# Block 5's low-half top-k search: from sign sums on ScalarE to counts on VectorE

## The chip, the cores and the metric

The kernel runs on one core of a Trainium2 chip. The metric is the device time of one execution in microseconds (us); smaller is better. The engines are TensorE (PE, matmul), VectorE (DVE), ScalarE (ACT), GpSimd (POOL) and SyncE (SP, which issues most DMAs).

## What is computed

One decoder layer over 1024 tokens of width 1024: a mixer of sparse attention and a gated short convolution, then a mixture of 32 experts with two per token. What matters here is the sparse attention. For each block of 128 query rows an indexer gives a score for every admissible key, and only the 256 best keys of each row take part in the softmax:

```python
score = jnp.where(admissible[None], score.astype(jnp.float32), -jnp.inf)
_, idx = lax.top_k(score, top_k)          # top_k = 256
...
logits = jnp.where(valid[:, :, None, None, :], logits, -jnp.inf)
p = jax.nn.softmax(logits, axis=-1)
```

Blocks 0 and 1 have at most 256 admissible keys and need no choice. Block t (2 to 7) has rows of 128 (t + 1) scores.

## The kernel before

The stages follow one another on TensorE: the projections and the indexer's scores (to about 190 us), twelve convolution columns and eight gate tiles (`conv_in`, `conv_out`, `gconv_tile`, to about 428 us), the attention of blocks 0 to 7, with the other gates' matmuls as filling (to about 640 us), the merge and the router, then the experts.

**The search.** `topk` does not sort. It finds the 256th largest score of each row as a bit pattern and then turns the score tile into a bias of 0 or -1e30. It has four steps: a 16-bit key from the upper half of each score; a descent over 16 bits on that key ("th"); the same on the lower half ("tl") among the scores whose upper half equals the one found; and the finish, which builds the threshold, breaks ties by a running count, and writes the bias over the scores. One bit of a descent counts, for each row, the keys at or above a candidate and moves the candidate up or down.

There are two searches. The vector search (blocks 2, 3, 4: 384, 512 and 640 scores) counts on VectorE with a compare that sums (line 357), then three short operations on [128, 3] tiles (lines 370 to 373). The tiles `acc` and `over` of these lie in PSUM, in a tile of tag "pv", which has one buffer. The scalar search (blocks 5, 6, 7: 768, 896 and 1024 scores) takes on ScalarE the sum of the signs of key minus candidate (line 328), and two one-column operations per block move the candidate (lines 343 and 347). Its keys, its finish and the preparation between the halves run on VectorE. The finish (lines 405 to 424) is VectorE's; its last operation, the write-back of the bias (line 426), is ScalarE's.

**Who sets the order.** In the convolution and gate stage the order of TensorE, VectorE and ScalarE is the order in which the program writes the instructions (`manual_schedule`). Both searches are generators. Ahead of each piece of work they yield its engine and an estimate of its length, and `search(us)` (line 430) takes pieces until the credit of the engines is used up:

```python
left = {n: us * SHARE[n] + searches.get(n, 0.0) for n in SHARE}
for name in ("scalar", "vector"):
    while name in searches:
        gen, step = searches[name]
        if step is not None:
            if left[step[0]] <= 0:
                break
            left[step[0]] -= step[1]
        step = next(gen, None)
```

An overdraft is carried to the next call, unused credit is not. `proj_col` calls `search(2.8)` in the middle and at the end of each of its two chains of 24 matmuls (four calls per column, none in the columns 0 and 1), and `gconv_tile` once more after each of its two up-projections, ahead of the gate product of line 530: six calls per gate tile. `SHARE` is 0.72 for VectorE, and for ScalarE 0.6 in the convolution part and 0.68 from the gate tiles on. What is left after the last call is written by one `search(1.0e6)` behind the stage, outside the fixed order and at low priority (`prio(LATE)`): the planner puts it where an engine has nothing else.

**After it.** In the attention only TensorE's order is fixed by hand; VectorE and ScalarE are ordered by the planner. `att_probs` reads the bias of its block, `att_values` transposes the probabilities, splits them into the tiles `ph` and `pl` (tag "pt", four buffers, which it shares with the search's `junk`, `signs` and the keys of blocks 6 and 7), and multiplies by the values into the PSUM tile `o`, which has the tag "pv" too.

Of the kernel before, what the change touches and what calls it, by code (L numbers as in the profile page):

```python
# [9 lines left out]
F32 = mybir.dt.float32  # L10
F32R = mybir.dt.float32r
I16 = mybir.dt.int16
U16 = mybir.dt.uint16
I32 = mybir.dt.int32
AF = mybir.ActivationFunctionType
OP = mybir.AluOpType
AX = mybir.AxisListType

P = 128
# [8 lines left out]
TOPK = 256  # L28
LN_EPS = 1e-5
ALPHA = 2.0 ** 0.25  # L30
NEG = -1.0e30
# [47 lines left out]
def build(tc, I, out):  # L79
    nc = tc.nc  # L80
# [73 lines left out]
    def psf(name, shape=(P, 512), tag="f", dt=F32):  # L154
        return ps.tile(list(shape), dt, name=name, tag=tag, bufs={"f": 2, "l": 3, "tr": 2, "pv": 1}[tag])
# [84 lines left out]
    for t in range(NB):  # L240
# [12 lines left out]
        c = slice(t * P, (t + 1) * P)  # L253
# [8 lines left out]
    score = {}  # L262
    w = load_nat("w_qi", 512, "wwcc")
    for t in range(2, NB):
# [8 lines left out]
        L = (t + 1) * P  # L273
        sc = kv.tile([P, L], F32, name=f"score{t}")
        score[t] = sc
        for h in range(NH):
            for n0 in range(0, L, 512):
# [8 lines left out]
                else:  # L286
                    nc.vector.scalar_tensor_tensor(sc[:, n0:n1], rl, wis[:, t, h:h + 1], sc[:, n0:n1],  # L287
                                                   op0=OP.mult, op1=OP.add)
# [12 lines left out]
    junk = part("junk", [P, S], "pt", 4, U16)  # L301
    keys = kv.tile([P, 18 * P], U16, name="keys")

    def topk(blocks, scalar=False):
        ng = len(blocks)
        V = nc.vector

        def tmp(name, dt=F32):
            return const.tile([P, ng], dt, name=f"{name}{blocks[0]}")

        cnt, acc, neg, sg, off, need = [tmp(n) for n in ("cnt", "acc", "neg", "sg", "off", "need")]
        if not scalar:
            pa = psf("acc", (P, 2 * ng), "pv")
            acc, over = pa[:, :ng], pa[:, ng:]
        hi, lo, msk = [tmp(n, I32) for n in ("thi", "tlo", "msk")]
        L = [(t + 1) * P for t in blocks]
        if scalar:
            key = [keys[:, 12 * P:12 * P + n] if n == 6 * P else part("key", [P, S], "pt", 4, U16)[:, :n] for n in L]
            signs = part("signs", [P, S], "pt", 4, I16)
            scratch = signs.bitcast(U16)  # L320
        else:
            key = [keys[:, sum(L[:i]):sum(L[:i + 1])] for i in range(ng)]
            scratch = junk

        def sign_sums(dt, b, o):
            for i in range(ng):
                yield "act", 0.45 + L[i] / 1000
                nc.scalar.activation(signs[:, :L[i]], key[i].bitcast(dt), AF.Sign, bias=b[:, i:i + 1], scale=1.0,
                                     accum_out=o[:, i:i + 1])

        def descend_signs(name, base, dt, above=None):

            c, b, total, sign, least = [tmp(name + n) for n in ("", "b", "s", "g", "l")]
            V.memset(b, 0.5 - (base + 32768.0))
            for i in range(ng):
                if above is None:
                    V.memset(least[:, i:i + 1], L[i] - 511.0)
                else:
                    V.tensor_scalar(least[:, i:i + 1], above[:, i:i + 1], 2.0 * L[i] - 511.0, None, op0=OP.add)
            for bit in range(15, -1, -1):  # L340
                yield from sign_sums(dt, b, total)
                for i in range(ng):
                    nc.scalar.activation(sign[:, i:i + 1], total[:, i:i + 1], AF.Sign, bias=least[:, i:i + 1],
                                         scale=1.0)
                if bit:
                    for i in range(ng):
                        nc.scalar.activation(b[:, i:i + 1], sign[:, i:i + 1], AF.Identity, bias=b[:, i:i + 1],
                                             scale=-float(1 << bit) / 2)
            yield "act", 2.0
            yield "act", 0.0  # L350
            V.scalar_tensor_tensor(c, sign, 0.5, b, op0=OP.mult, op1=OP.subtract)
            return c

        def count(op, dt, c, o):
            for i in range(ng):
                yield "dve", 0.4 + L[i] / 1000
                V.tensor_scalar(junk[:, :L[i]], key[i].bitcast(dt), c[:, i:i + 1], None, op0=op, op1=OP.add,
                                accum_out=o[:, i:i + 1])

        def descend(name, base, dt, above=None):  # L360
            if scalar:
                return (yield from descend_signs(name, base, dt, above))
            c = tmp(name)
            if above is not None:
                V.tensor_copy(over, above)
            V.memset(c, base + 32768.0)
            for bit in range(15, -1, -1):
                yield from count(OP.is_ge, dt, c, cnt)
                if above is not None:
                    V.tensor_tensor(cnt, cnt, over, op=OP.add)  # L370
                step = float(1 << bit)
                V.tensor_scalar(acc, cnt, TOPK - 0.5, step, op0=OP.is_ge, op1=OP.mult)
                V.scalar_tensor_tensor(c, acc, -step / 2 if bit else -1.0, c, op0=OP.add, op1=OP.add)
            return c

        for i, t in enumerate(blocks):
            yield "dve", L[i] / 500
            h = score[t].bitcast(I16)[:, 1::2]
            m = scratch[:, :L[i]].bitcast(I16)
            V.tensor_scalar(m, h, 0.0, 32767.0, op0=OP.is_lt, op1=OP.mult)  # L380
            V.tensor_tensor(key[i].bitcast(I16), h, m, op=OP.bitwise_xor)
        th = yield from descend("th", -32768.0, I16)
        above = tmp("above")
        if scalar:
            V.tensor_scalar(acc, th, -1.0, -0.5, op0=OP.mult, op1=OP.add)
            yield from sign_sums(I16, acc, above)
            yield "act", 2.0
            yield "act", 0.0
        else:
            yield from count(OP.is_gt, I16, th, above)  # L390
        V.tensor_scalar(neg, th, 0.0, None, op0=OP.is_lt)
        V.tensor_scalar(sg, neg, -2.0, 1.0, op0=OP.mult, op1=OP.add)
        V.tensor_scalar(off, neg, 65535.0, None, op0=OP.mult)
        for i, t in enumerate(blocks):
            low = score[t].bitcast(U16)[:, 0::2]
            yield "dve", L[i] / 400
            V.tensor_scalar(scratch[:, :L[i]], low, sg[:, i:i + 1], off[:, i:i + 1], op0=OP.mult, op1=OP.add)
            V.scalar_tensor_tensor(key[i], key[i].bitcast(I16), th[:, i:i + 1], scratch[:, :L[i]], op0=OP.is_equal,
                                   op1=OP.mult)
        if scalar:  # L400
            yield "act", 2.0
            yield "act", 0.0
        tl = yield from descend("tl", 0.0, U16, above)
        yield "dve", 1.5
        V.tensor_copy(hi, th)
        V.tensor_scalar(msk, neg, 32767.0, None, op0=OP.mult)
        V.tensor_tensor(hi, hi, msk, op=OP.bitwise_xor)
        V.tensor_scalar(hi, hi, 16, None, op0=OP.logical_shift_left)
        V.tensor_tensor(tl, tl, sg, op=OP.mult)
        V.tensor_tensor(lo, tl, off, op=OP.add)  # L410
        V.tensor_tensor(hi, hi, lo, op=OP.bitwise_or)
        for i, t in enumerate(blocks):
            s = score[t]
            T = hi.bitcast(F32)[:, i:i + 1]
            jk, cm = scratch[:, :L[i]], key[i]
            yield "dve", L[i] / 300
            V.tensor_scalar(jk, s, T, None, op0=OP.is_gt, op1=OP.add, accum_out=cnt[:, i:i + 1])
            V.tensor_scalar(jk, s, T, None, op0=OP.is_equal)
            yield "dve", L[i] / 300
            V.tensor_scalar(need[:, i:i + 1], cnt[:, i:i + 1], -1.0, float(TOPK), op0=OP.mult, op1=OP.add)  # L420
            V.tensor_tensor_scan(cm, jk, jk, 0.0, op0=OP.add, op1=OP.bypass)
            yield "dve", L[i] / 300
            V.scalar_tensor_tensor(cm, cm, need[:, i:i + 1], jk, op0=OP.is_le, op1=OP.mult)
            V.scalar_tensor_tensor(s, s, T, cm, op0=OP.is_gt, op1=OP.add)
            yield "act", L[i] / 800
            nc.scalar.activation(s, s, AF.Copy, bias=NEG, scale=-NEG)

    searches = {}

    def search(us):  # L430

# [266 lines left out]
    for i in range(FILLEND):  # L698
        const_w = MINFILL if i >= 8 else MINFILL0
        if i < len(units):  # L700
            L = (units[i][0] + 1) * P
# [121 lines left out]
    V = nc.vector  # L823
# [196 lines left out]
    raw, parts, xT, gu, act, hT = {}, {}, {}, {}, {}, {}  # L1020
# [397 lines left out]
def pack(inputs):  # L1418
# [4 lines left out]
    def tiled(m):  # L1423
        return c(m.reshape(-1, P, m.shape[1]).transpose(1, 0, 2))

    o = {}
    o["x"] = c(a["x"][0])
    o["xt"] = tiled(a["x"][0].T)
    o["w_q"] = tiled(w[:, 0:512])
# [12 lines left out]
    o["w_out"] = tiled(a["w_out"][0])  # L1442
    o["gate_bias"] = c(a["gate_bias"][0].reshape(16, P).T)
    o["conv_w"] = c(a["conv_w"][0].reshape(3, 4, P).transpose(2, 1, 0))
# [30 lines left out]
```

## Time and profile before

| | us |
|---|---|
| median of 3 runs (1473.53 to 1477.25) | 1474.6 |
| the profiled execution | 1478.14 |
| its span, first to last instruction | 1476.3 |
| TensorE busy | 1399.8 (95%) |
| VectorE busy | 1092.0 (74%) |
| ScalarE busy | 996.0 (67%) |
| GpSimd busy | 395.1 (27%) |

All rows of the trace are of the one profiled execution, and times within it count from the start of its span. A row of a timeline gives the start, the length, the engine, the line, the operation and its tiles, and in brackets how long the engine stood idle before it and what released it. A row of a group gives the busy time in total, the mean of one in ns, and the idle time before. The granted clock of TensorE is given as a share of full speed.

### The profile page before, as it was taken

How to read it: one execution, taken by the hardware profiler on the slowest of the kernel's cores; microseconds unless marked ns; L12 is line 12 of the kernel's file. 1: busy time of each engine (PE TensorE's matmuls, PEld its weight loads, DVE VectorE, ACT ScalarE, POOL GpSimd, SP SyncE). 2: the span in 40 equal slices, each digit the busy share in tenths (PEclk: the TensorE clock that was granted, in tenths of full speed). 3: DMA queues.
4: the chain of work that ended last, by engine and by line, in shares of the span. 5: the costliest groups of instructions: out<-in, count | busy, mean ns of one | idle time of the engine just before them, and what ended most of it. 6: DMA issues, size and time to landing. Idle time of an engine off the chain costs nothing.

```text
span 1476.3 us, 20415 instructions
## 1 busy us (share of the span) xinstructions
PE 1399.8 (95%) x6746; PEld 1154.8 (78%) x6746; DVE 1092.0 (74%) x1917; ACT 996.0 (67%) x1657; POOL 395.1 (27%) x343
## 2 busy tenths in 40 slices
PE   8999999999979999998999799999999999999993
PEld 7888688878867888886887688888887787777772
DVE  5354699995066666677526799999999888888876
ACT  5453468779936766675323488888888788778864
POOL 2442113232224555541000212211111111111106
PEclk9999999999989999999999699999999999999997
DMA  5211111122121121247746688999999999999942
GB/s 197 72 43 57 59 57 44 46 84 79 44 85 58 58 72 65 86 165 251 273 160 240 251 290 320 369 370 369 359 365 360 357 354 360 366 358 363 365 188 115
DMA packets 97054, 301.78 MB, mean 204 GB/s; under 512 B 14671, under 2 KB 19151, under 8 KB 96945
## 3 DMA queue, kind: packets, MB, share of 16 engines
q1 hardware_dynamic: 88160, 284.28, 52.3%
q0 software_dynamic: 8784, 16.16, 4.3%
q8 instruction: 54, 0.88, 0.2%
q14 instruction: 56, 0.45, 0.1%
HBM read 276.12 MB, written 40.11 MB: 214 GB/s over the span
## 4 chain that ended last, share of the span: by engine, by line
PE 66%; DMA 15%; DVE 9%; ACT 5%; issue 3%; POOL 1%; SPq 0%; ACTq 0%; DVEq 0%; POOLq 0%
DMA er<-in_w_e 13%; PE pc L148 6%; PE pc L150 6%; PE pc L149 6%; PE gu L148 4%; PE gu L150 4%; PE gu L149 4%; PE pj L148 2%; PE pj L149 2%; PE pj L150 2%; PE py L1113 2%; PE py L1117 2%; PE py L1114 2%; PE pv L664 2%; DVE el L139 2%
## 5 line engine op out<-in xcount | busy, mean ns | idle before, releaser
L139 DVE TENSOR_TENSOR el<-er,eh 128x1024 fp32r<-128x1024 f32 x376 | 442.9, 1220 | 47.1 <-ACT eh L135 44.6
L135 ACT ACTIVATE eh<-er 128x1024 fp32r<-128x1024 f32 x376 | 385.9, 1062 | 48.8 <-PE gu L150 17.4
L148 PE MATMUL gu<-eh,exh 128*128 128x512 f32 x512 | 209.0, 408 | 0.0
L150 PE MATMUL gu<-eh,exl 128*128 128x512 f32 x512 | 203.4, 397 | 0.0
L149 PE MATMUL gu<-el,exh 128*128 128x512 f32 x512 | 203.2, 397 | 0.0
L148 PE MATMUL pc<-xh,ch 128*128 128x512 f32 x448 | 178.8, 399 | 0.0
L150 PE MATMUL pc<-xh,cl 128*128 128x512 f32 x448 | 175.7, 392 | 0.0
L149 PE MATMUL pc<-xl,ch 128*128 128x512 f32 x448 | 175.4, 392 | 0.0
L1134 POOL DMA_INDIRECT y_d<-yo,gidx x29 | 46.1, 1588 | 436.5 <-ACT yo L1126 421.9
L150 PEld LDWEIGHTS gu<-eh,exl 128*128 128x128 f32 x512 | 96.8, 189 | 23.8 <-DVE exl L139 0.5
L148 PEld LDWEIGHTS gu<-eh,exh 128*128 128x128 f32 x512 | 97.1, 190 | 20.7 <-ACT exh L135 0.4
L149 PEld LDWEIGHTS gu<-el,exh 128*128 128x128 f32 x512 | 97.1, 190 | 20.4
L139 POOL TENSOR_TENSOR cl<-cr,ch 128x1024 fp32r<-128x1024 f32 x28 | 68.1, 2431 | 134.4 <-ACT ch L135 115.2
L1114 PE MATMUL py<-el,hT 128*128 128x512 f32 x256 | 101.3, 396 | 0.0
L1113 PE MATMUL py<-eh,hT 128*128 128x512 f32 x256 | 101.3, 396 | 0.0
L150 PEld LDWEIGHTS pc<-xh,cl 128*128 128x128 f32 x448 | 84.5, 189 | 18.1
L645 POOL TENSOR_TENSOR p<-p,mx 128x128 f32<-128x128 f32 (+7 forms) x64 | 74.8, 1179 | 82.0 <-DVE mx L644 75.3
L148 PEld LDWEIGHTS pc<-xh,ch 128*128 128x128 f32 x448 | 84.7, 189 | 13.5 <-ACT rl L283 0.4
L149 PEld LDWEIGHTS pc<-xl,ch 128*128 128x128 f32 x448 | 84.7, 189 | 13.4
L287 DVE SCALAR_TENSOR_TENSOR score<-rl,wis,score 128x512 f32<-128x512 f32 (+1 forms) x70 | 53.6, 779 | 44.8 <-ACT rl L283 43.7
L1117 PE MATMUL py<-eh,hT 128*128 128x512 f32 x256 | 80.3, 395 | 0.0
L283 ACT ACTIVATE rl<-sc 128x512 f32<-128x512 f32 (+1 forms) x80 | 41.1, 524 | 53.7 <-PE sc L281 41.3
(338 smaller groups left out, 3032.4 us busy)
## 6 DMA issues: line engine op xcount, KB each, us to landing
er<-in_w_e SPq DMA_DIRECT2D x384, 512.0 KB, 11.1
cr<-in_w_ct SPq DMA_DIRECT2D x28, 512.0 KB, 3.5
gc_d<-g SPq DMA_DIRECT2D x8, 512.0 KB, 2.6
ga_d<-g SPq DMA_DIRECT2D x8, 512.0 KB, 2.6
gg<-ga_d SPq DMA_DIRECT2D x16, 256.0 KB, 4.0
gg<-gc_d SPq DMA_DIRECT2D x16, 256.0 KB, 4.4
wor<-in_w_out SPq DMA_DIRECT2D x8, 512.0 KB, 5.4
xn<-in_x SPq DMA_DIRECT2D x8, 512.0 KB, 4.8
```

What stands on the lines that cost most here:

```text
L135: exps["last"] = nc.scalar.activation(hi, src, AF.Copy).ins
L139: i = eng.tensor_tensor(lo, src, hi.bitcast(F32), op=OP.subtract)
L148: nc.tensor.matmul(ps, sh, mh, start=start, stop=False)
L149: nc.tensor.matmul(ps, sh, ml, start=False, stop=False)
L150: return nc.tensor.matmul(ps, sl, mh, start=False, stop=stop).ins
L283: nc.scalar.activation(rl, a, AF.Relu)
L287: nc.vector.scalar_tensor_tensor(sc[:, n0:n1], rl, wis[:, t, h:h + 1], sc[:, n0:n1], op0=OP.mult, op1=OP.add)
L645: nc.gpsimd.tensor_tensor(p[:, :L], p[:, :L], mx[:, 0:1].to_broadcast([P, L]), op=OP.mult)
L1113: nc.tensor.matmul(py[n], hT[e][:, 0, k], hi[k][:, cs], start=k == 0, stop=False)
L1114: nc.tensor.matmul(py[n], hT[e][:, 0, k], lo[k][:, cs], start=False, stop=False)
L1117: nc.tensor.matmul(py[n], hT[e][:, 1, k], hi[k][:, cs], start=False, stop=k == 3)
L1134: nc.gpsimd.indirect_dma_start(out=y_d, out_offset=bass.IndirectOffsetOnAxis(ap=si, axis=0), in_=yo, in_offset=None, bounds_check=S - 1, o ...
```

## The change

The low half of block 5's search leaves the scalar search. `descend_signs` and `sign_sums` get a first block `i0`, and the low half now runs with `i0 = 1`, for blocks 6 and 7 alone. A new `descend_one` does block 5's low half by counts on VectorE, one column wide, with `acc` and `over` in a PSUM tile of tag "pv" and `junk` as the output of its compare. The finish becomes a function `finish(tl, i0, i1, scratch)` over a range of blocks. The scalar search appends a generator `first_alone` (block 5's counts and finish) to a list, and the vector search runs it after its own finish. The upper half of block 5 stays on ScalarE.

```diff
+        def descend_one(base, dt, above, c):
+
+            pa = psf("acc", (P, 2), "pv")
+            acc, over = pa[:, 0:1], pa[:, 1:2]
+            cnt, c = tmp("cnt1")[:, 0:1], c[:, 0:1]
+            V.tensor_scalar(over, above[:, 0:1], float(L[0]), 0.5, op0=OP.add, op1=OP.mult)
+            V.memset(c, base + 32768.0)
+            for bit in range(15, -1, -1):
+                yield "dve", 0.7 + L[0] / 1000
+                V.tensor_scalar(junk[:, :L[0]], key[0].bitcast(dt), c, None, op0=OP.is_ge, op1=OP.add,
+                                accum_out=cnt)
+                V.tensor_tensor(cnt, cnt, over, op=OP.add)
+                step = float(1 << bit)
+                V.tensor_scalar(acc, cnt, TOPK - 0.5, step, op0=OP.is_ge, op1=OP.mult)
+                V.scalar_tensor_tensor(c, acc, -step / 2 if bit else -1.0, c, op0=OP.add, op1=OP.add)
...
-        tl = yield from descend("tl", 0.0, U16, above)
-        yield "dve", 1.5
...
+        def finish(tl, i0, i1, scratch):
+            r = slice(i0, i1)
+            yield "dve", 1.5
...
+            for i in range(i0, i1):
...
+                yield "dve", L[i] / 300
...
+                yield "act", L[i] / 800
+                nc.scalar.activation(s, s, AF.Copy, bias=NEG, scale=-NEG)
+
+        if not scalar:
+            tl = yield from descend("tl", 0.0, U16, above)
+            yield from finish(tl, 0, ng, scratch)
+            yield from shared[0]
+            return
+
+        def first_alone():
+            tl = tmp("tf")
+            yield from descend_one(0.0, U16, above, tl)
+            yield from finish(tl, 0, 1, junk)
+
+        shared.append(first_alone())
+        tl = yield from descend_signs("tl", 0.0, U16, above, 1)
+        yield from finish(tl, 1, ng, scratch)
 
-    searches = {}
+    searches, shared = {}, []
```

## Rows read from the trace of the kernel before

**Rows 1.** Page, section 2: busy tenths in 40 slices, TensorE and VectorE.

```profile
PE   8999999999979999998999799999999999999993
...
DVE  5354699995066666677526799999999888888876
```

**Rows 2.** Busy us by stretch: length, PE, PEld, DVE, ACT, POOL; clock, DMA, GB/s.

```profile
352.00:409.00 57.00, 57.00 (x258) 47.11 (x257) 5.18 (x11) 52.83 (x134) 15.28 (x11) 1.00 0.17 62
...
431.00:442.00 11.00, 3.28 (x9) 2.04 (x9) 9.95 (x26) 4.23 (x12) 3.54 (x4) 0.57 0.34 119
...
440.00:450.00 10.00, 8.52 (x35) 6.98 (x36) 6.15 (x29) 4.50 (x14) 4.88 (x9) 0.69 0.00 0
```

**Rows 3.** TensorE's timeline around the hole: start, length, operation, wait and releaser.

```profile
434.51 0.48 PE L633 MATMUL lg<-kT,qT 128*128 128x128 f32 x1 [3.89 <-DVE mx L635]
...
439.93 0.47 PE L672 MATMUL tr<-identr,p 128*128 128x128 f32 x1 [3.34 <-POOL p L645]
...
442.21 0.58 PE L664 MATMUL pv<-ph,vhl 128*128 128x256 f32 x1 [0.15 <-ACT ph L135]
```

**Rows 4.** VectorE's timeline in the same stretch, long operations.

```profile
425.28 0.69 DVE L530 TENSOR_TENSOR g<-pu,g 128x512 f32<-128x512 f32 x1 [6.62 <-PE pu L150]
...
428.00 3.38 DVE L423 SCALAR_TENSOR_TENSOR key<-key,need,signs 128x896 uint16<-128x896 uint16 x1
...
431.31 0.68 DVE L530 TENSOR_TENSOR g<-pu,g 128x512 f32<-128x512 f32 x1
...
431.91 1.14 DVE L424 SCALAR_TENSOR_TENSOR score<-score,thi,key 128x896 f32<-128x896 f32 x1
...
432.96 1.27 DVE L417 TENSOR_SCALAR_CACHE_REDUCE signs<-score,thi 128x1024 uint16<-128x1024 f32 x1
...
435.91 2.28 DVE L421 TENSOR_TENSOR_SCAN key<-signs 128x1024 uint16<-128x1024 uint16 x1
...
439.65 1.30 DVE L424 SCALAR_TENSOR_TENSOR score<-score,thi,key 128x1024 f32<-128x1024 f32 x1
```

**Rows 5.** ScalarE: write-backs of blocks 3, 4, 2 (timeline); block 5's low sums (groups).

```profile
345.27 0.61 ACT L426 ACTIVATE score<-score 128x512 f32<-128x512 f32 x1
...
351.56 0.74 ACT L426 ACTIVATE score<-score 128x640 f32<-128x640 f32 x1 [2.50 <-DVE score L424]
...
406.77 0.52 ACT L426 ACTIVATE score<-score 128x384 f32<-128x384 f32 x1
...
L328 ACT ACTIVATE signs<-keys,tlb 128x768 int16<-128x768 uint16 x16 | 14.8, 924 | 8.0 <-DVE tll L339 8.0
```

**Rows 6.** VectorE's timeline: one low-half bit of the vector search.

```profile
285.17 0.62 DVE L357 TENSOR_SCALAR_CACHE_REDUCE junk<-keys,tl 128x384 uint16<-128x384 uint16 x1
...
287.54 0.16 DVE L370 TENSOR_TENSOR cnt<-cnt,acc 128x3 f32<-128x3 f32 x1
...
288.13 0.61 DVE L357 TENSOR_SCALAR_CACHE_REDUCE junk<-keys,tl 128x384 uint16<-128x384 uint16 x1
```

**Rows 7.** VectorE's groups by shape, 190 to 436 us: busy us, mean ns.

```profile
L357 DVE TENSOR_SCALAR_CACHE_REDUCE junk<-keys,tl 128x384 uint16<-128x384 uint16 x16 | 9.8, 612 | 0.5
...
L357 DVE TENSOR_SCALAR_CACHE_REDUCE junk<-keys,tl 128x640 uint16<-128x640 uint16 x16 | 14.0, 877 | 0.4
...
L417 DVE TENSOR_SCALAR_CACHE_REDUCE signs<-score,thi 128x768 uint16<-128x768 f32 x1 | 1.0, 1012 | 0.0
...
L418 DVE TENSOR_SCALAR signs<-score,thi 128x768 uint16<-128x768 f32 x1 | 0.6, 621 | 0.0
```

**Rows 8.** VectorE's timeline, finish of block 6, with the gate product ahead of it.

```profile
408.96 0.69 DVE L530 TENSOR_TENSOR g<-pu,g 128x512 f32<-128x512 f32 x1 [12.89 <-PE pu L150]
...
409.57 0.15 DVE L351 SCALAR_TENSOR_TENSOR tl<-tlg,tlb 128x3 f32<-128x3 f32 x1
...
415.86 1.02 DVE L424 SCALAR_TENSOR_TENSOR score<-score,thi,keys 128x768 f32<-128x768 f32 x1
```

**Rows 9.** What TensorE waited for from 442 to 640 us: total, times, longest.

```profile
PE pv L664 <- ACT ph L135: 2.8, 5, 1.2
```

More of the change, by code (lines that the diff above doesn't have):

```diff
@@ L323, in topk, with sign_sums @@
             scratch = junk
-        def sign_sums(dt, b, o):
-            for i in range(ng):
+        def sign_sums(dt, b, o, i0=0):
+            for i in range(i0, ng):
                 yield "act", 0.45 + L[i] / 1000
@@ L329, in sign_sums, with descend_signs @@
                                      accum_out=o[:, i:i + 1])
-        def descend_signs(name, base, dt, above=None):
+        def descend_signs(name, base, dt, above=None, i0=0):
             c, b, total, sign, least = [tmp(name + n) for n in ("", "b", "s", "g", "l")]
             V.memset(b, 0.5 - (base + 32768.0))
-            for i in range(ng):
+            for i in range(i0, ng):
                 if above is None:
@@ L340, in descend_signs @@
             for bit in range(15, -1, -1):
-                yield from sign_sums(dt, b, total)
-                for i in range(ng):
+                yield from sign_sums(dt, b, total, i0)
+                for i in range(i0, ng):
                     nc.scalar.activation(sign[:, i:i + 1], total[:, i:i + 1], AF.Sign, bias=least[:, i:i + 1],
@@ L345, in descend_signs @@
                 if bit:
-                    for i in range(ng):
+                    for i in range(i0, ng):
                         nc.scalar.activation(b[:, i:i + 1], sign[:, i:i + 1], AF.Identity, bias=b[:, i:i + 1],
@@ L350, in descend_signs @@
             yield "act", 0.0
-            V.scalar_tensor_tensor(c, sign, 0.5, b, op0=OP.mult, op1=OP.subtract)
+            V.scalar_tensor_tensor(c[:, i0:], sign[:, i0:], 0.5, b[:, i0:], op0=OP.mult, op1=OP.subtract)
             return c
@@ L402, in topk @@
             yield "act", 0.0
-        tl = yield from descend("tl", 0.0, U16, above)
-        yield "dve", 1.5
[L405 to L426, printed above, removed]
@@ L428, in build @@
-    searches = {}
+        def finish(tl, i0, i1, scratch):
+            r = slice(i0, i1)
+            yield "dve", 1.5
+            V.tensor_copy(hi[:, r], th[:, r])
+            V.tensor_scalar(msk[:, r], neg[:, r], 32767.0, None, op0=OP.mult)
+            V.tensor_tensor(hi[:, r], hi[:, r], msk[:, r], op=OP.bitwise_xor)
+            V.tensor_scalar(hi[:, r], hi[:, r], 16, None, op0=OP.logical_shift_left)
+            V.tensor_tensor(tl[:, r], tl[:, r], sg[:, r], op=OP.mult)
+            V.tensor_tensor(lo[:, r], tl[:, r], off[:, r], op=OP.add)
+            V.tensor_tensor(hi[:, r], hi[:, r], lo[:, r], op=OP.bitwise_or)
+            for i in range(i0, i1):
+                s = score[blocks[i]]
+                T = hi.bitcast(F32)[:, i:i + 1]
+                jk, cm = scratch[:, :L[i]], key[i]
+                yield "dve", L[i] / 300
+                V.tensor_scalar(jk, s, T, None, op0=OP.is_gt, op1=OP.add, accum_out=cnt[:, i:i + 1])
+                V.tensor_scalar(jk, s, T, None, op0=OP.is_equal)
+                yield "dve", L[i] / 300
+                V.tensor_scalar(need[:, i:i + 1], cnt[:, i:i + 1], -1.0, float(TOPK), op0=OP.mult, op1=OP.add)
+                V.tensor_tensor_scan(cm, jk, jk, 0.0, op0=OP.add, op1=OP.bypass)
+                yield "dve", L[i] / 300
+                V.scalar_tensor_tensor(cm, cm, need[:, i:i + 1], jk, op0=OP.is_le, op1=OP.mult)
+                V.scalar_tensor_tensor(s, s, T, cm, op0=OP.is_gt, op1=OP.add)
+                yield "act", L[i] / 800
+                nc.scalar.activation(s, s, AF.Copy, bias=NEG, scale=-NEG)
```

## Prediction

> **What bounds the kernel now.** I began with the busy strips of the page: TensorE stands at nine tenths or more in slices 1 to 10 and 12 to 17, with one dip between, at slice 11, while VectorE is half empty in slice 9 and empty in slice 10 [rows 1]. So the two searches are normally covered by TensorE's own work, and an edit to them counts only where TensorE waits for them. The busy times by stretch show where that is. From 352 to 409 us TensorE is busy for all 57.0 us, ScalarE for 52.8 and VectorE for only 5.2. From 431 to 442 us TensorE has 3.28 busy us of 11, at a granted clock of 0.57, while VectorE is busy for 9.95. From 440 to 450 us the clock is still 0.69 [rows 2].
>
> The timeline of TensorE in that hole shows the first attention units: a wait of 3.89 us at 434.51 for VectorE's row maxima, a wait of 3.34 us at 439.93 for the normalised probabilities, and the first value product (line 664) at 442.21 [rows 3]. VectorE's timeline says why: it still runs the end of the search there. The product with the gates at 431.31 stands behind a search step of 3.38 us, then come the write-back of block 6 at 431.91, the count of block 7 at 432.96, the scan of block 7 at 435.91 and its write-back at 439.65, with the attention's short operations squeezed between them [rows 4]. So the end of the search sets the end of this one stretch and of nothing else near it. That is the place where the change can pay, and where it can hurt.
>
> **Where the moved work lands.** `search` hands out the steps of both generators: each call adds 2.8 x 0.68 = 1.904 us of ScalarE credit and 2.8 x 0.72 = 2.016 us of VectorE credit (from the gate tiles on), the scalar search is served first, and a generator stops at a step whose engine has no credit. There are 40 calls in the convolution part and 48 (numbers 41 to 88) in the eight gate tiles. What is left after call 88 is emitted at low priority outside the fixed order.
>
> Before: the low half of the scalar search starts at call 47 and takes 48 sums, 16 x (1.218 + 1.346 + 1.474) = 64.6 us of credit, so it ends at call 82. Until then ScalarE's credit is always used up by it, and so the vector search sticks at its first ScalarE step, the write-back of block 2. The trace bears this out: that write-back (128x384) runs at 406.77, long after those of blocks 3 and 4 at 345.27 and 351.56, which were left for the low-priority end and so could be put earlier [rows 5].
>
> After: 32 sums are 16 x (1.346 + 1.474) = 45.1 us of credit, so the low half ends at call 70, eleven calls earlier. On ScalarE 16 sums of 0.924 us go [rows 5], but TensorE waits for ScalarE nowhere between 352 and 409 us [rows 2], so this gives nothing by itself. At call 71 the vector search gets past its step; but now VectorE's credit goes first to the finish of blocks 6 and 7 (1.5 + 3 x 2.987 + 3 x 3.413 = 20.7 us), then to that of blocks 3 and 4 (3 x 1.707 + 3 x 2.133 = 11.5 us): 32.2 / 2.016 = 16 calls, 71 to 85 with the overdraft allowed. The 16 new counting steps (1.468 us of credit each) begin only in call 86. Calls 86, 87 and 88 take one each. Thirteen steps and the finish of block 5 are left for the low-priority end. So the idle VectorE time of 352 to 409 us is not what the counts use.
>
> **What the left-over holds up.** `descend_one` keeps its counts in `acc` and `over`, a PSUM tile of tag "pv", which has one buffer; the next user of that buffer is `o`, the target of the attention's first value product. TensorE's order is fixed by hand, so that product, which ran at 442.21 [rows 3], and all behind it wait until the sixteenth step is done. Before, the vector search gave the buffer back with its last count, ahead of the write-backs at 345 and 351 us [rows 5], so this is a new wait.
>
> Price of a step: in the vector search a low-half bit runs from 285.17 to 288.13, that is 2.96 us, of which the three short operations from 287.54 on take 0.59 [rows 6]. The counts cost 0.612 us at 384 elements and 0.877 at 640, 0.133 per 128 more; extended to 768 that is 1.01, and the compare-and-count of line 417 at 768 takes 1.012 [rows 7]. With the read of the accumulator and the gap to the next one (1.06 from start to start) a step of the new search is 1.06 + 0.59 = 1.65 us. The operands of the short operations lie as before; one column in place of three I price the same.
>
> The three steps of the fixed order: between the gate products of tile 6 (the first at 408.96 [rows 8]) and that at 425.28, which waits for TensorE [rows 4], VectorE has block 4 to finish and two counting steps (3.3 us). Block 6's finish takes 6.6 us [rows 8] and block 4 is smaller, so both fit. The third step can start only behind it, at 425.9. From there 14 steps x 1.65 = 23.1 us, plus the last gate product 0.6, plus the attention's own short operations that come before the first value product. VectorE's 9.95 us of 431 to 442 less the four long search operations shown there (1.14, 1.27, 2.28, 1.30) leave 4.0 as their upper end, with zero as the lower; I take 2.6, since part of the 4.0 is search too [rows 2, 4]. So the buffer comes free at 425.9 + 23.1 + 0.6 + 2.6 = 452.2, against 442.2 for the product before: +10.0 us (between +7.4 and +11.4). The hole is longer but TensorE is at the lower clock behind it in both kernels [rows 2]; I count nothing for that, between -1 and +1.
>
> Then the finish of block 5 is still to come. The finish of a block of 768 elements (15 operations of line 351 and lines 405 to 424) runs from 409.57 to 416.88 with one gate product of 0.7 between, 6.6 us [rows 8]. It is of low priority, but VectorE works in order and steps of 1.0 to 1.8 us lie among the attention's short ones; it also holds one of the four "pt" buffers in which ScalarE and VectorE put the transposed probabilities. From zero to 6.6, I take 1.5, since VectorE has 35 to 40% idle from 440 us on (6.15 busy of 10 [rows 2]).
>
> Gain: a call is worth (425.28 - 408.96) / 6 = 2.7 us [rows 4, 8], so the finish of blocks 6 and 7, whose last call is 79 in place of the end, is out of the way by about 400 us; the waits of 3.89 and 3.34 us go. They are not to be subtracted: the product they led to now waits for the later event anyway. The sum is +11.5 us. From 442 to 640 us TensorE's waits for other engines are few (the largest total is 2.8 us [rows 9]), and the filling matmuls stand in a fixed order, so nothing there can take the delay back; the later loads start when this stage frees their buffers, so I carry it whole to the end, 0 to 2 us less as the lower bound. The profiled execution is 1478.14 us with a span of 1476.3, so it becomes 1489.6; against the median of 1474.6 the forecast is 1486.1.
>
> **A rule against a row.** The counts rise by 0.133 us per 128 elements, 1.04 ns for one [rows 7]. By the Trainium skill, "VectorE: DVE Perf Modes", section "The perf-mode tier table", a tensor_scalar on 16-bit data in SBUF reaches four elements per cycle; an estimate from that page's clock would make the count some 0.6 us shorter than one by the row, and the new search some 8 us shorter (1478 in all). The trace does not agree for the form that also sums, so the sum above goes by the row; a milder version in rows is the fourth rival.
>
> **The rivals.**
> First, the same mechanism with the longer release: if the buffers of tag "pt" are handed out in turn, the first transposed probabilities get that of `junk`, which the finish of block 5 still uses. Then the first value product waits for the finish up to its second-last long step too, 6.6 - 1.0 = 5.6 us more, and the 1.5 above falls away: 1474.6 + 10.0 + 5.6 = 1490.2. For it: no row shows by what rule the four buffers are handed out. Against: the three others are free by about 400 us, with the finish of blocks 6 and 7. Chance 0.15.
> Second, the other side: the counts run in the idle stretch of 352 to 409 us (16 x 1.65 = 26.4 us in 52 idle ones [rows 2]) and all is done by 425. It holds if the vector search is not stopped at its ScalarE step. Then the waits of 3.89 and 3.34 us [rows 3] go, and the first value product comes at 435 to 436 in place of 442.2: some 6 us sooner, 1468.5. Against it stands the write-back at 406.77 [rows 5]. Chance 0.09.
> Third, the placing is right but the product does not wait for the PSUM buffer: the earlier finish of blocks 6 and 7 gives up to 6 us, and 28 us of low-priority work under the first blocks of the attention takes some of it back: 1469 to 1477, in the middle 1473. Against: the code gives that tag one buffer. Chance 0.08.
> Fourth, cheaper counts: at the 0.621 us of a compare of 768 elements that doesn't sum [rows 7] a step is 0.39 shorter, 14 steps 5.5: 1486.1 - 5.5 = 1480.6. Against: every count of the trace. Chance 0.04.
> That nothing is changed in the schedule is excluded by the credit sums above.
>
> **How the numbers follow.** The forecast has 0.64, and the rivals have 0.15, 0.09, 0.08 and 0.04. The forecast's own bounds are 7.4 + 0 - 1 to 11.4 + 6.6 + 1 at their corners; taken together sensibly 1480.5 to 1491. The range adds the first and the fourth rival: 1480 to 1492. It leaves out the second and third, 0.17. A measurement can tell 0.3% (4.4 us) from no change, so slower means above 1479.0: 0.64 + 0.15 + 0.04 = 0.83. Faster means below 1470.2: the second rival, 0.09. The rest, 0.08, is within.
>
> **What would show it.** Right: the last sums of blocks 6 and 7 on ScalarE end near 377 us (eleven calls of 2.7 us before 406.77); block 7's write-back on VectorE lies near 400; thirteen counting steps of about 1.65 us stand behind 427 us; the first value product starts at about 452 and names a VectorE step of the new search as what it waited for; the lengthened hole is the only large difference. Wrong: counts between 352 and 409 us; a first value product before 442; a wait for ScalarE's transposed probabilities instead (the first rival); steps clearly under 1.6 us; or a later stage that takes the delay back.

## The result and the profile after

| kernel | median us | profiled execution us | its span us |
|---|---|---|---|
| before | 1475.27 (6 runs) | 1478.14 | 1476.3 |
| after | 1483.71 (6 runs) | 1486.61 | 1484.8 |

The ratio after to before is 1.0062, with a 95% interval of 1.0051 to 1.0073: 8.4 us slower. The forecast was 1486.1 us within 1480 to 1492.

Begin where [rows 1 and 2] began. In the strips of the page (slices counted from 0) VectorE's slice 10 has gone from 0 to 5, which is the finish of blocks 6 and 7 moved forward; slice 9 from 5 to 2 and slice 11 from 6 to 8, since the finish of blocks 3 and 4 now lies at 400 to 417 us; TensorE's dip at slices 11 and 12 has deepened from 7 and 9 to 6 and 7. The busy times by stretch (columns as in [rows 2]) say the same in us.

```profile
PE   8999999999967999998999699999999999999993
...
DVE  5354699992587666668634789998999898888976
```

```profile
352.00:409.00 57.00, 57.00 (x257) 47.09 (x256) 22.29 (x36) 31.30 (x70) 15.56 (x11) 1.00 0.12 42
431.00:442.00 11.00, 0.99 (x5) 0.57 (x4) 10.34 (x49) 2.62 (x10) 1.92 (x5) 0.63 0.20 70
440.00:450.00 10.00, 0.00 (x0) 0.00 (x0) 9.13 (x32) 0.00 (x0) 0.00 (x0) 0.50 0.00 0
```

From 352 to 409 us ScalarE has 31.30 busy us where it had 52.83, VectorE 22.29 where it had 5.18, and TensorE is fully busy in both. So nothing was gained there. From 440 to 450 us TensorE does nothing at all, and VectorE is busy for 9.13 of the 10 us. TensorE's timeline, to set beside [rows 3], shows why:

```profile
431.73 0.33 PE L704 MATMUL tr<-identr,p 128*128 128x128 f32 x1 [0.68 <-POOL p L677]
433.59 0.33 PE L704 MATMUL tr<-identr,p 128*128 128x128 f32 x1 [1.53 <-POOL p L677]
450.46 0.55 PE L696 MATMUL pv<-ph,vhl 128*128 128x256 f32 x1 [16.25 <-DVE tf L374]
```

The wait of 3.89 us for the row maxima is gone, the first transposition waits 0.68 us where it had waited 3.34, and the second waits 1.53. In their place stands one wait of 16.25 us: the first value product (line 696 now) waits for line 374, the last operation of a step of the new search. VectorE's timeline has the steps themselves (line 369 is the count, 562 the gate product, 434 to 441 the finish), to set beside [rows 4, 8]:

```profile
378.77 0.72 DVE L351 SCALAR_TENSOR_TENSOR tl<-tlg,tlb 128x2 f32<-128x2 f32 x1
...
399.14 1.28 DVE L441 SCALAR_TENSOR_TENSOR score<-score,thi,key 128x1024 f32<-128x1024 f32 x1
...
417.39 1.01 DVE L369 TENSOR_SCALAR_CACHE_REDUCE junk<-keys,tf 128x768 uint16<-128x768 uint16 x1
...
424.74 0.69 DVE L562 TENSOR_TENSOR g<-pu,g 128x512 f32<-128x512 f32 x1 [4.11 <-PE pu L150]
425.35 1.00 DVE L369 TENSOR_SCALAR_CACHE_REDUCE junk<-keys,tf 128x768 uint16<-128x768 uint16 x1
...
426.97 1.01 DVE L369 TENSOR_SCALAR_CACHE_REDUCE junk<-keys,tf 128x768 uint16<-128x768 uint16 x1
...
447.08 1.01 DVE L369 TENSOR_SCALAR_CACHE_REDUCE junk<-keys,tf 128x768 uint16<-128x768 uint16 x1
...
448.71 1.01 DVE L369 TENSOR_SCALAR_CACHE_REDUCE junk<-keys,tf 128x768 uint16<-128x768 uint16 x1
...
450.15 0.16 DVE L374 SCALAR_TENSOR_TENSOR tf<-acc,tf 128x1 f32<-128x1 f32 x1
...
452.86 1.75 DVE L438 TENSOR_TENSOR_SCAN keys<-junk 128x768 uint16<-128x768 uint16 x1
...
457.56 1.36 DVE L441 SCALAR_TENSOR_TENSOR score<-score,thi,keys 128x768 f32<-128x768 f32 x1
```

Two counts lie ahead of the gate product at 424.74, fourteen from 425.35 to 450.31, 1.63 us from start to start (447.08 to 448.71). The product on TensorE starts 0.15 us behind the last one. Then the finish of block 5 runs among the attention's short operations until 458.9.

For the rest three stages were read in every kernel's profiled execution, each from starts in the trace. A is from the attention's first logit product (tile `lg`) to its first value product (tile `pv`). B is from the same start to the last value product. C is from the first to the last transposition of an expert's tokens (tile `etr`, at 833.1 and 1400.2 in before), far behind the attention. The medians of before lay between 1474.73 and 1476.06 in the sessions; the ratios are each against the runs of the same one.

| kernel | median us | ratio to before (95%) | A | B | C |
|---|---|---|---|---|---|
| before | 1475.27 | 1 | 13.8 | 231.0 | 567.1 |
| after | 1483.71 | 1.0062 (1.0051 to 1.0073) | 22.6 | 242.1 | 564.6 |
| e1_sums_in_sbuf | 1474.9 | 0.9997 (0.998 to 1.0013) | 7.2 | 232.1 | 563.4 |
| e2_counts_early | 1463.43 | 0.9912 (0.9888 to 0.9935) | 5.5 | 222.6 | 565.1 |
| e3_before_free_yield | 1475.16 | 0.9987 (0.9974 to 1.0) | 13.8 | 230.5 | 567.1 |
| e4_twelve_bits | 1478.89 | 1.0018 (1.0005 to 1.0031) | 16.0 | 236.0 | 563.8 |
| e5_no_finish5 | 1483.04 | 1.0053 (1.0031 to 1.0074) | 22.6 | 240.2 | 564.4 |
| e6_more_vector_credit | 1477.86 | 1.0024 (1.0012 to 1.0037) | 6.3 | 222.2 | 565.1 |
| e7_counts_before_finish | 1465.35 | 0.9937 (0.9917 to 0.9956) | 5.5 | 223.0 | 564.0 |
| e8_counts_early_again | 1463.91 | 0.9928 (0.9911 to 0.9944) | 5.5 | 222.6 | 564.1 |
| e9_before_two_tiles | 1473.76 | 0.9984 (0.9971 to 0.9997) | 13.8 | 232.1 | 564.8 |
| e10_no_new_tiles | 1487.74 | 1.0083 (1.0066 to 1.0099) | 22.6 | 241.9 | 565.9 |

### The profile page after: what moved, and what is told of

It reads as the page before. It is cut to its first block, busy times and chain, and to the rows that moved or that the text cites. A ratio compares the mean times of both kernels' runs of the same rounds, so it can differ in the third digit from the quotient of the medians.

```text
span 1484.8 us, 20440 instructions
## 1 busy us (share of the span) xinstructions
PE 1399.3 (94%) x6746; PEld 1155.7 (78%) x6746; DVE 1112.5 (75%) x2005; ACT 975.5 (66%) x1594; POOL 396.4 (27%) x343
## 4 chain that ended last, share of the span: by engine, by line
PE 34%; DMA 11%; DVE 5%; ACT 2%; issue 1%; SPq 0%; ACTq 0%; DVEq 0%
DMA er<-in_w_e 10%; PE gu L150 5%; PE gu L148 5%; PE gu L149 5%; PE py L1145 3%; PE py L1149 3%; PE py L1146 3%; PE mix L148 2%; PE mix L149 2%; PE mix L150 2%; DVE el L139 1%; PE etr L1105 1%; DVE yr L1375 1%; PE pj L1015 1%; PE etr L1134 1%
```

## The experiments

**Is it the PSUM buffer?** In after, the two sums of the new search go into SBUF:

```
-            pa = psf("acc", (P, 2), "pv")
+            pa = tmp("acc1")
```

> The changed kernel with one thing other: acc and over of descend_one lie in a small SBUF tile, not in the PSUM buffer of tag pv. The counts stay where they are (three steps in the fixed order, thirteen behind it). Theory (the first value product waits for the PSUM buffer): it then starts when the transposed probabilities are there, at 434 to 436 us in place of 450.5, and the wait of 16.25 us is gone; the left-over 23 us of VectorE steps lie under the first attention blocks and cost some of it: 1470 to 1478 us. Rival A (the buffers of tag pt, by junk, or VectorE itself hold the first units up): the first value product stays at 445 us or later and the time within 3 us of 1483.7.

TensorE's timeline, first value product:

```profile
433.48 0.58 PE L696 MATMUL pv<-ph,vhl 128*128 128x256 f32 x1 [0.15 <-ACT ph L135]
```

The wait is gone, with the search left where it was; A falls from 22.6 to 7.2 us. So the buffer, and not VectorE's load, held the product. But the last fourteen steps of the search now run among the operations of the first attention units, from 423.8 to 463.1 us, and B is no shorter than before's (232.1 against 231.0). The time is that of before: without the wait the change's loss is gone, but nothing is gained, since the work is still in the wrong place.

**Is it where the credit puts the counts?** The write-back step of blocks 2, 3 and 4, on which the vector search sticks while ScalarE has no credit, is made free; the scalar search's own stays:

```
-                yield "act", L[i] / 800
+                yield ("act", L[i] / 800) if scalar else ("dve", 0.0)
```

> The changed kernel with one yield other: the write-back in the finish of the vector search no longer waits for ScalarE credit (it yields a VectorE step of length 0). By the credit sums block 5's counts then begin in call 63 in place of 86 and end in call 84, all but the last write-back inside the fixed order. Theory: the first value product starts at 434 to 437 us, ahead of the kernel before (442.2), and the time is 1466 to 1471 us, faster than before by 0.3 to 0.6%. Rival A (VectorE, now busy from 352 us on, holds up the gate products or the attention): TensorE shows new waits before 428 us or the product stays at 442 us or later, 1475 us or more. Rival B (the hole is set by the attention's own start): product at 440 to 442, 1474 to 1476.

> The same kernel as the one with the counts early (the write-back step of blocks 2 to 4 made free of credit), once more and longer, for its interval. Theory: the same as there, 1462 to 1465, ratio 0.990 to 0.993, first value product 5 to 6 us behind the first gate-logit product. Rival (the 12.6 us found there held some 4 us of chance, since attention itself gained only 8.4): 1466 to 1469.

By the credit sums the counts now begin in call 63 and end in call 84. The busy times by stretch of e2 and the first value product of e8, in that order:

```profile
352.00:409.00 57.00, 57.00 (x258) 47.05 (x257) 40.36 (x101) 29.17 (x64) 13.91 (x10) 1.00 0.13 47
431.00:442.00 11.00, 10.26 (x53) 8.69 (x53) 6.65 (x36) 6.28 (x21) 4.06 (x9) 0.84 0.02 8
```

```profile
432.97 0.40 PE L696 MATMUL pv<-ph,vhl 128*128 128x256 f32 x1 [0.30 <-ACT ph L135]
```

VectorE's idle stretch has taken the counts (40.36 busy us, TensorE still at 57.0), and the hole in TensorE is closed: 10.26 busy us of 11 where before had 3.28. The product came at 431.3 in e2 and the time at 1463.43, both better than I had expected. This kernel beats before, by 0.9% and in the longer set by 0.7%. The longer set's rival, 1466 to 1469, falls. Its gain of 10.8 us is about B's 8.4 and C's 3.0; C is looked at below.

**Does the free step alone do it?** The same edit in the kernel before (where line 425 holds the step):

> The kernel before with the same one yield changed as in e2_counts_early and nothing else. Theory: the finish of blocks 3 and 4 already ran early there, and the end of the scalar search (call 82, then the finish of blocks 5, 6 and 7) is not moved, so the hole of 431 to 442 us stays and the time is that of before, 1473 to 1477 us. Rival: the yield alone frees the end of the search, the first value product comes before 438 us and the time falls below 1471 us; then a gain of e2_counts_early is not the change's.

A stays at 13.8, and the ratio's interval reaches 1.0. The step pays only with block 5's low half off ScalarE; before, the finish of blocks 6 and 7 was what came last.

**Does each step on VectorE carry over to the product?** The loop of the new search is cut short; its last four steps are left out:

```
-            for bit in range(15, -1, -1):
+            for bit in range(15, 3, -1):
```

> The changed kernel with the last four of descend_one's sixteen steps left out (block 5's low half is then found to 12 bits only). Theory: the chain of steps of 1.63 us each sets the first value product, so it starts 4 x 1.63 = 6.5 us sooner, at 444 us, and the time falls by about 6 us to 1477 to 1479 us. Rival (something else releases it, such as the finish of block 5 or the attention's own chain): the product moves by less than 3 us and the time by less than 3 us.

TensorE's waits (total, times, longest), 442 to 640 us:

```profile
PE pv L696 <- DVE tf L374: 9.7, 1, 9.7
```

The wait shrinks by 16.25 - 9.67 = 6.58 us, four steps of 1.633 are 6.53. The time falls by 4.8 us, or by 6.5 if each kernel is set against before in its own session.

**What does the finish of block 5 cost?** In after, the call of that finish is taken out:

```
-            yield from finish(tl, 0, 1, junk)
```

> The changed kernel without the finish of block 5 (fifteen VectorE operations and one ScalarE operation of the low-priority end are left out, so block 5's keep-mask is never made). My theory: the sixteen counting steps alone hold the first value product, and the finish costs about 2.3 us more behind it (first gate-logit product to last value product is 242.1 us in the changed kernel, 8.8 longer than before up to the first value product and 2.3 longer behind it). So the first value product stays 22.6 us (22 to 23) behind the first gate-logit product, the stage from there to the last value product ends 1.5 to 3 us sooner, and the time is 1480.5 to 1482.5 against 1483.7. Rival one (the longer release: the finish holds the first value product too): the wait of 16.25 us gets 3 to 6 us shorter and the time falls below 1480. Rival two (the finish is hidden; the 2.3 us behind the product are something else): nothing moves, 1483 to 1484.5.

A stays at 22.6, which refutes the first rival: the product doesn't wait for the finish. B is 1.9 us shorter, so the finish costs about that; e9 below, whose attention is before's own, has a B 1.1 us off before's, so the figure is rough. The total moved by only 0.7 us against an expected 1.2 to 3.2, 1483.04 lies in the second rival's range, and the two intervals overlap; the total can't decide it.

**Does more credit place them as well?** One line is added to after, behind the one that sets ScalarE's share in the gate tiles:

```
         SHARE["act"] = 0.68
+        SHARE["dve"] = 1.2
```

> The changed kernel with VectorE's share in the gate tiles raised from 0.72 to 1.2, so each call gives 3.36 us of VectorE credit in place of 2.016; nothing else differs. My theory (credit places the steps): the credit sums then put the first counting step into call 79, the last into call 86, and block 5's finish into calls 86 to 88; nothing is left for the low-priority end. The steps begin near 400 us once the finish of blocks 6, 7 and 4 is through, sixteen of 1.63 us with two gate products end near 430, and the finish, now in the fixed order ahead of the attention's row maxima, near 436: first value product 438 to 443 (11 to 16 us behind the first gate-logit product, against 22.6), wait for the last counting step gone, time 1470 to 1477. Rival (credit does not place them; VectorE simply has no room before 425): counts still end near 450 and the time stays at 1482 to 1485. If the earlier part of the search gets in the way of TensorE's gate tiles, the first gate-logit product comes later than 428 and shows it.

The wait for the counts is gone as expected, but the first value product came at 450.97, not at 438 to 443, and the time is just above its range. TensorE's waits, TensorE's timeline and VectorE's timeline show a wait in another place:

```profile
PE pc L148 <- DVE g L562: 7.6, 1, 7.6
```

```profile
443.32 0.76 PE L148 MATMUL pc<-xh,ch 128*128 128x512 f32 x1 [7.60 <-DVE g L562]
```

```profile
440.84 1.76 DVE L438 TENSOR_TENSOR_SCAN keys<-junk 128x768 uint16<-128x768 uint16 x1
442.51 0.67 DVE L562 TENSOR_TENSOR g<-pu,g 128x512 f32<-128x512 f32 x1
```

The first count started at 411.00, not near 400, because the finishes of blocks 3 and 4 both still lay ahead of it and I had allowed for one. Counts and finish, now in the fixed order, push a gate product back to 442.51, and TensorE's next tile waits for that. The first logit product slips from 427.9 to 444.7. Credit places the steps, but credit that VectorE can't honour moves the hole from the attention into the gate tiles.

**Is it the counts' place, or the early finish of blocks 2 to 4?** In after the chain is moved ahead of the vector search's own finish:

```
             tl = yield from descend("tl", 0.0, U16, above)
-            yield from finish(tl, 0, ng, scratch)
             yield from shared[0]
+            yield from finish(tl, 0, ng, scratch)
```

> The changed kernel with the chain moved by one line: the vector search goes from its last bit straight into block 5's counts and finish, and the finish of blocks 2, 3 and 4, with the ScalarE step on which it sticks, comes behind them. Every operation is kept. My theory: the credit sums then start the sixteen steps in call 55 and end them in call 66, between about 335 and 366 us, with sums of blocks 6 and 7 running beside them on ScalarE, and block 4's finish is the last of the search, in calls 86 to 88, near 428. So nothing is left for the low-priority end, the wait for the counting steps is gone, the first value product comes 5 to 8 us behind the first gate-logit product, and the time is 1462 to 1468, as with the step that was made free. Rival (the gain of that kernel came from blocks 2 to 4 being finished early, not from the counts running in the idle stretch): block 4's finish at the end costs 5 us at the value product and the time is 1469 to 1475.

VectorE's timeline, first and last count, and TensorE's, first value product:

```profile
334.45 1.02 DVE L369 TENSOR_SCALAR_CACHE_REDUCE junk<-keys,tf 128x768 uint16<-128x768 uint16 x1
...
364.00 1.01 DVE L369 TENSOR_SCALAR_CACHE_REDUCE junk<-keys,tf 128x768 uint16<-128x768 uint16 x1
```

```profile
433.85 0.39 PE L696 MATMUL pv<-ph,vhl 128*128 128x256 f32 x1 [0.30 <-ACT ph L135]
```

The counts lie where the credit sums had put them, and block 4's finish ends at 427.6; A is 5.5 and B 223.0, as with the free step. The rival falls: it is the counts' place.

**What comes back behind the attention?** C is 567.1 us in before and in e3, and 563.4 to 565.1 in after and its first seven variants, whether their attention was late or early. Two runs ask whether two new tiles of constants, which shift what is allocated behind them, do that. In the first, before gets them unused; in the second, after does without (`cnt1` becomes `cnt`, and `tl = tmp("tf")` becomes `tl = need`):

```
+        if scalar:
+            V.memset(tmp("cnt1"), 0.0)
+            V.memset(tmp("tf"), 0.0)
         tl = yield from descend("tl", 0.0, U16, above)
```

> The kernel before with two more tiles of twelve bytes a partition in the pool of constants (named as the two that the change adds, each cleared once and not used); nothing else differs. What it is for: from the first to the last transposition of an expert's tokens the kernel before and its variant take 567.1 us, the changed kernel and its seven variants 563.4 to 565.1, so some 2.5 us come back behind the attention whether that was late or early. Theory A (placing: the two tiles shift what is allocated behind them by 24 bytes): that stage takes 563.5 to 565.2 us here too, attention is as before (first gate-logit product to last value product 230.5 to 231.5), and the time is 2 to 3.5 us under before, 1471 to 1473. Theory B (it comes from the order of the work or of the loads): the stage stays at 567 and the time at 1474 to 1476.

> The changed kernel with the two new constant tiles taken away: the count goes into the search's existing count tile and the descent into the tile that later holds the needed number, so no tile is added; the work and its order are the same. Theory A (placing): the expert stage, first to last transposition of tokens, goes back to 566.5 to 567.5 us and the time rises to 1485.5 to 1488, with the first value product still 22 to 23 us behind the first gate-logit product. Theory B (order): stage 563.4 to 565.1 and time 1483 to 1485, as in the changed kernel.

C, with its first and last start, by the tile view of `etr` in e9 and then in e10:

```profile
L1076 PE MATMUL etr<-identr,xg x256: 270/272/444, 831.3 to 1396.1; 128*128 128x128 f32 x128
```

```profile
L1105 PE MATMUL etr<-identr,xg x256: 270/272/448, 844.8 to 1410.7; 128*128 128x128 f32 x128
```

In e9 the tiles, each cleared once, bring C to 564.8, as placing would have it; the time (1473.76) lies between the two theories' ranges. In e10 C comes back to only 565.9, between the theories. Its time is 4 us above that of after, but the intervals of the two ratios overlap, and of the 2.3 us by which their profiled executions differ 1.2 lie ahead of the attention. Each C is one execution's, and e2 and e8, which are the same kernel, differ by 1.0 us in it. So e9 speaks for placing, and e10 doesn't settle it. What shortens C, by how much and by what mechanism, stays open.

## Why the prediction was right

**The credit sums** held to the call. ScalarE's last sums of blocks 6 and 7 end at 375.7 us (forecast: near 377), and ScalarE's timeline has block 2's write-back 30 us sooner than in [rows 5]:

```profile
374.44 1.15 ACT L328 ACTIVATE signs<-key,tlb 128x1024 int16<-128x1024 uint16 x1
375.49 0.19 ACT L328 ACTIVATION_READ_ACCUMULATOR signs<-key,tlb 128x1 f32 x1
...
376.90 0.51 ACT L443 ACTIVATE score<-score 128x384 f32<-128x384 f32 x1
```

Block 7's write-back on VectorE stands at 399.14 (forecast: near 400). Two counts lie ahead of the last gate tile, the third starts at 425.35 (425.9), and the other thirteen follow from 426.97 (behind 427).

**The PSUM buffer** was the wait, and e1 shows it by itself. The third rival, no wait, falls with it, and the first (the longer release) with e5. The second, counts in the idle stretch, did not happen in after; e2, e7 and e8 show what it is worth: 9 to 13 us less than before, some 3 of them C's, where the rival's price was 6.

**The step** measured 1.63 us against 1.65. By the prediction's estimate from the Trainium skill, "VectorE: DVE Perf Modes", section "The perf-mode tier table", the count would be some 0.6 us shorter. The trace doesn't agree for the form that also sums: 1.01 us at 768 elements of 16 bits, 0.133 more than the 0.877 at 640 in [rows 7]. The fourth rival falls by the same row.

**The terms that were off.** The product was to come 10.0 us later. A grew by 8.8. Against the forecast 452.2 the measured 450.46 is 1.74 sooner: 0.55 by the start (0.5 of that is the whole execution's, whose first logit product is at 427.9 in place of 428.4), 0.2 by the step, and 1.1 because the attention's short operations ahead of the product take 1.5 us and not 2.6 (24.96 us from 425.35 to 450.31, less 14 x 1.633, less 0.6 for the gate product), with 0.15 back for the gap to the product. The finish was to cost 1.5; from the first to the last value product after takes 2.3 us more than before, and 1.9 go when the finish is left out. That makes 8.8 + 2.3 = 11.1 at the end of the attention, where 11.5 was forecast: two errors that nearly cancel, so that the sum is closer than its terms by luck.

**The step that failed** is "I carry it whole to the end, 0 to 2 us less". At the end 8.4 us are left. C in before and then in after:

```profile
L1073 PE MATMUL etr<-identr,xg x256: 270/272/444, 833.1 to 1400.2; 128*128 128x128 f32 x128
```

```profile
L1105 PE MATMUL etr<-identr,xg x256: 270/272/448, 843.8 to 1408.4; 128*128 128x128 f32 x128
```

C is 2.5 us shorter in after, and 11.1 - 2.5 = 8.6. The prediction allowed for up to 2 us, and only as a delay that is taken back. That it is a delay taken back is not what the runs show: C is as short in e2 and e8, whose attention is early. A shorter C came with every form of the change's code, and the prediction had no term for it; e9 points to the two tiles, e10 leaves the cause open.

## What to carry to other kernels

Work that a budget hands out late is not moved into the idle time that it was meant for: replay the budget call by call, and ask at which step the generator sticks. When the place is found, list which scarce buffers the moved work holds, and who wants them next. Two edits that each looked neutral or bad (the moved counts, the free step) gave 0.7 to 0.9% together, since the one opened the room and the other let the work into it.

## What the runs showed of the hardware

Some VectorE operations with two SBUF tensors as inputs were about three times as long where a GpSimd operation started beside them. VectorE's timeline and GpSimd's in e7, and the same operation alone in e6 (groups by shape, mean ns at the end):

```profile
377.54 3.20 DVE L441 SCALAR_TENSOR_TENSOR score<-score,thi,keys 128x768 f32<-128x768 f32 x1
```

```profile
377.53 2.40 POOL L139 TENSOR_TENSOR cl<-cr,ch 128x1024 fp32r<-128x1024 f32 x1 [7.80 <-ACT ch L135]
```

```profile
L441 DVE SCALAR_TENSOR_TENSOR score<-score,thi,keys 128x768 f32<-128x768 f32 x1 | 1.0, 1019 | 0.0
```

It took 3.20 us in place of 1.02 beside a GpSimd operation of 2.40. The search step of 3.38 us in [rows 4] is such a case too: the same operation on 896 elements takes 1.15 alone in e6 (at 388.32). The Trainium skill, "GPSIMD Engine Reference", section "1. Specifications", names this contention for VectorE instructions with two SBUF inputs; these rows agree. It did not strike every neighbour: in after the operation of that line at 384.50 kept its 1.15 us, and the GpSimd operation that started 0.37 us behind it took 1.96, where others of its shape take 1.30. Nor are two SBUF tensors needed: a compare of 384 elements that doesn't sum took 1.45 us at 335.39 in after, beside a GpSimd operation of 1.30, and 0.42 alone at 410.13 in e7. The counts, with one SBUF tensor as input, showed no such stretch: 1.00 to 1.02 us each, in e7 also where the GpSimd operations of 346.28 and 352.11 run beside them. And in e9 twenty-four bytes more of constants a partition, unused, went with an expert stage 2.3 us shorter 400 us later; whether they caused it is open (e10).
